# A feed-forward input product as 2x2 blocks with seven block products in place of eight, in a one-core encoder kernel

## The chip, the core and the metric

The kernel runs on one core of a Trainium2 chip. A core has TensorE (PE, matrix products; its weight loads are listed as PEld), VectorE (DVE), ScalarE (ACT), GpSimd (POOL) and SyncE (SP), which run their own instruction lists in order and wait for each other through semaphores. SP issues plain loads and stores; POOL issues, besides its arithmetic, the transfers that add to what lies at the destination. Products accumulate in PSUM banks of 128 x 512 fp32. The metric is the device time of one execution in microseconds (us).

## The reference, cut to what matters

Two layers. Each has a token mixer, a cross-attention and a SwiGLU feed-forward, each followed by a layer norm of ALPHA * x plus the branch. The change touches the norm after the cross-attention and the feed-forward:

```python
D_MODEL, SEQ, DEPTH = 1024, 512, 2
FFN_HIDDEN = 2816

def swiglu_ffn(x, w_in, w_down):          # x (512, 1024)
    gu = x @ w_in                         # w_in (1024, 2 * 2816)
    g, up = gu[..., :FFN_HIDDEN], gu[..., FFN_HIDDEN:]
    return (jax.nn.silu(g) * up) @ w_down
...
        y = memory_cross_attention(x, mem, xa_w_q[l], xa_w_kv[l], xa_w_o[l])
        x = layer_norm(ALPHA * x + y, ln2_g[l], ln2_b[l])
        y = swiglu_ffn(x, ffn_w_in[l], ffn_w_down[l])
        x = layer_norm(ALPHA * x + y, ln3_g[l], ln3_b[l])
```

## The kernel before

All products are fp32 made of three products of rounded parts: each operand is split into `hi` (rounded to fp32r) and `lo` (the rest), and `mm3` issues hi x hi, hi x lo and lo x hi into one PSUM region (lines 250 to 252, so these three lines carry nearly all matmuls).

**The input product of the feed-forward** is 44 blocks a layer (22 gates and 22 ups, alternating). A `Block` has 128 hidden columns: its weights are one tile of 128 x 1024, eight pieces of 128 x 128 that stand in the array while the transposed activations `xT` (128 x 512 tokens) stream through. A block is 8 x 3 = 24 matmuls of 512 columns into one bank. Its weights come in four steps (`added_weights`, lines 282 to 290): SP loads the raw tile, ScalarE rounds it to `whi`, ScalarE writes -`whi` to `wlo`, and a POOL transfer adds the raw weights from DRAM onto `wlo`. The first three blocks make `lo` on VectorE instead (`split`). After a gate ScalarE takes its tanh and VectorE combines; after an up VectorE writes the product to `hid`.

**Buffers.** `wring` has 7 `whi` and 7 `wlo` tiles (RING), `rawp` 3 raw tiles, `big` 26 tiles of 4 KB a partition (x, xT, hid, gains and others), `s2` 9 scratch tiles. PSUM: 4 `accb` banks, and 4 more that `psb` hands out in turn (3 `psb`, 1 `convb`). A tile's slot is fixed when the kernel is built, and whoever writes a slot first waits for the last reader of the tile before it.

**The tail of the cross-attention** (`tail`, lines 509 to 531) adds the last output products to x token tile by token tile (4 tiles of 128), norms, and transposes x on TensorE: two groups of four 128 x 128 transposes a tile, each split by ScalarE and VectorE into `xTh` and `xTl`. x stays in SBUF until the norm after the feed-forward. The first halves (256 tokens) of three blocks are computed between the last transposes.

**The order.** In these stages the instructions' order on each engine is chosen when the kernel is built, by the tool's list scheduler, from the order in which the code is written and the tool's own estimates; at run time each engine follows its list strictly.

After the input product comes the output product of the feed-forward (`wlo<-in_fdn`, `hs`), 22 steps of 24 matmuls of 512 columns, which reads its weights in the same four steps.

## Time and profile before

| | |
|---|---|
| median of 3 runs | 1489.69 us (1489.43 to 1490.8) |
| the profiled execution | 1493.32 us, its span 1491.4 us |
| PE busy | 1453.1 us, 97% |
| DVE, ACT, POOL busy | 47%, 48%, 31% |
| HBM | 213.31 MB read, 8.39 MB written |

Busy times are of the whole span and average over stages with different limits: what the change is worth is read from the stage of the input product, which a layer has once. Where an engine's idle time is named, the releaser behind the arrow is what ended it. Matmuls overlap in the records: what counts for their rate is the distance between two starts, not the duration of one.

### The profile page before, as it was taken

Reading aid. Unit: us, or ns where it says so; the run is one execution under the profiler, and the core shown is the slowest. Engines: PE = TensorE matmul, PEld = TensorE weight load, DVE = VectorE, ACT = ScalarE, POOL = GpSimd, SP = SyncE. Lnnn points to the kernel's source line nnn. Section 1 sums busy time; section 2 is a strip of 40 time slices with the busy share of each in tenths; the row PEclk is TensorE's granted clock in tenths of the full one; section 3 lists DMA queues with packets and bytes.
Section 4 is the critical chain, followed back from the end, with each engine's and each line's share of the span. In section 5 each row is a group of like instructions: output and inputs, shape, how many; then the busy total and the mean of one; then the engine's idle time right before and its main releaser. Section 6 shows DMA issues by size and latency. Waiting matters only on the chain.

```text
span 1491.4 us, 21169 instructions
## 1 busy us (share of the span) xinstructions
PE 1453.1 (97%) x8152; PEld 1256.3 (84%) x8152; DVE 707.6 (47%) x1187; ACT 721.8 (48%) x1278; POOL 466.8 (31%) x665
## 2 busy tenths in 40 slices
PE   8799999999999999999999999999999999999997
PEld 7699988987988888888889999888889888888886
DVE  6999677665511111220469886685663111114005
ACT  3667773453544444553146777624525444446430
POOL 2679771000311111111148877410012111111111
PEclk9899999999999999999999999999999999999999
DMA  5325444242598888998433444423419888889871
GB/s 179 127 70 171 114 128 156 78 161 73 141 223 193 193 196 192 221 201 193 118 116 122 130 127 127 156 71 100 156 48 236 196 190 194 194 193 219 196 140 57
DMA packets 64452, 227.27 MB, mean 152 GB/s; under 512 B 7328, under 2 KB 7360, under 8 KB 64352
## 3 DMA queue, kind: packets, MB, share of 16 engines
q1 hardware_dynamic: 43616, 150.75, 31.1%
q0 software_dynamic: 20736, 75.17, 27.8%
q8 instruction: 64, 1.05, 0.3%
q14 instruction: 36, 0.29, 0.1%
HBM read 213.31 MB, written 8.39 MB: 149 GB/s over the span
## 4 chain that ended last, share of the span: by engine, by line
PE 75%; DVE 12%; ACT 5%; DMA 4%; POOL 3%; issue 1%; SPq 0%; POOLq 0%; DVEq 0%; ACTq 0%
PE accb L250 18%; PE accb L251 18%; PE accb L252 18%; PE psb L250 5%; PE psb L251 5%; PE psb L252 5%; DVE convb L628 3%; DMA raw<-in_xo 3%; DVE wlo L226 1%; DVE p L858 1%; DMA raw<-in_xq 1%; ACT whi L225 1%; PE convb L250 1%; PE convb L252 1%; PE convb L251 1%
## 5 line engine op out<-in xcount | busy, mean ns | idle before, releaser
L250 PE MATMUL accb<-xTh,whi 128*128 128x512 f32 (+1 forms) x1104 | 400.6, 365 | 1.5 <-ACT whi L225 1.3
L251 PE MATMUL accb<-xTl,whi 128*128 128x512 f32 (+1 forms) x1104 | 401.0, 364 | 0.5 <-DVE xTl L432 0.5
L252 PE MATMUL accb<-xTh,wlo 128*128 128x512 f32 (+1 forms) x1104 | 400.3, 363 | 0.1
L287 ACT CAST whi<-raw 128x1024 fp32r<-128x1024 f32 x126 | 132.7, 1055 | 339.4 <-PE accb L251 255.6
L250 PEld LDWEIGHTS accb<-xTh,whi 128*128 128x128 f32 x1104 | 208.7, 190 | 35.7 <-ACT xTh L429 2.7
L251 PEld LDWEIGHTS accb<-xTl,whi 128*128 128x128 f32 x1104 | 209.9, 190 | 32.9 <-DVE xTl L432 1.7
L252 PEld LDWEIGHTS accb<-xTh,wlo 128*128 128x128 f32 x1104 | 209.7, 190 | 32.5 <-DVE wlo L226 0.4
L289 POOL DMA_DIRECT2D wlo<-in_fin x82 | 71.0, 866 | 345.9 <-ACT wlo L288 336.6
L322 POOL TENSOR_TENSOR wlo<-raw,whi 128x1024 fp32r<-128x1024 f32 (+1 forms) x63 | 152.3, 2420 | 62.1 <-ACT whi L314 61.9
L1098 DVE SCALAR_TENSOR_TENSOR scr<-scr,accb 128x512 f32<-128x512 f32 x44 | 30.3, 688 | 253.4 <-ACT scr L1097 253.4
L628 DVE SCALAR_TENSOR_TENSOR convb<-ch,hvec,convb 128x511 f32<-128x511 f32 (+9 forms) x180 | 132.3, 735 | 5.2 <-ACT convb L625 1.7
L288 ACT ACTIVATE wlo<-whi 128x1024 fp32r<-128x1024 f32 x126 | 133.2, 1057 | 2.2
L226 DVE TENSOR_TENSOR wlo<-raw,whi 128x1024 fp32r<-128x1024 f32 (+1 forms) x49 | 56.5, 1158 | 127.2 <-ACT whi L225 126.4
L446 POOL TENSOR_SCALAR ve<-mv 128x1 f32<-128x1 f32 x32 | 27.5, 859 | 244.5 <-DVE mv L467 235.4
L289 POOL DMA_DIRECT2D wlo<-in_fdn x44 | 38.0, 863 | 198.4 <-ACT wlo L288 193.1
L1100 DVE SCALAR_TENSOR_TENSOR hid<-scr,accb 128x512 f32<-128x512 f32 x44 | 30.2, 687 | 136.7 <-PE accb L252 136.7
L225 ACT CAST whi<-raw 128x1024 fp32r<-128x1024 f32 (+1 forms) x49 | 48.9, 1002 | 84.9 <-PE accb L252 33.3
L619 POOL TENSOR_TENSOR cs<-cs,scr 128x511 f32<-128x511 f32 (+29 forms) x60 | 71.5, 1191 | 35.7 <-ACT scr L617 34.5
L314 ACT CAST whi<-raw 128x1024 fp32r<-128x1024 f32 (+1 forms) x63 | 66.7, 1060 | 4.6 <-PE accb L252 1.7
L250 PE MATMUL accb<-whi,hs 128*128 128x512 f32 x176 | 68.6, 390 | 0.0
L251 PE MATMUL accb<-wlo,hs 128*128 128x512 f32 x176 | 68.5, 389 | 0.0
L252 PE MATMUL accb<-whi,hs 128*128 128x512 f32 x176 | 68.5, 389 | 0.0
(295 smaller groups left out, 3165.8 us busy)
## 6 DMA issues: line engine op xcount, KB each, us to landing
raw<-in_fin SPq DMA_DIRECT2D x88, 512.0 KB, 3.6
wlo<-in_fin POOLq DMA_DIRECT2D x82, 512.0 KB, 5.6
raw<-in_fdn SPq DMA_DIRECT2D x44, 512.0 KB, 4.1
wlo<-in_fdn POOLq DMA_DIRECT2D x44, 512.0 KB, 5.9
raw<-in_xk SPq DMA_DIRECT2D x16, 512.0 KB, 3.6
raw<-in_xv SPq DMA_DIRECT2D x16, 512.0 KB, 3.6
raw<-in_wo SPq DMA_DIRECT2D x16, 512.0 KB, 3.6
raw<-in_xq SPq DMA_DIRECT2D x16, 512.0 KB, 3.6
```

What stands on the lines that cost most here:

```text
L225: nc.scalar.copy(hi, src)
L226: nc.vector.tensor_tensor(lo, src, hi.bitcast(F32), op=ALU.subtract)
L250: nc.tensor.matmul(o, l[0], r[0], start=first, stop=False)
L251: nc.tensor.matmul(o, l[0], r[1], start=False, stop=False)
L252: nc.tensor.matmul(o, l[1], r[0], start=False, stop=last)
L287: nc.scalar.copy(hi[:, :1024], raw[:, :1024])
L288: nc.scalar.activation(lo[:, :1024], hi[:, :1024].bitcast(F32), AF.Copy, scale=-1.0)
L289: nc.gpsimd.dma_start(out=lo[:, :1024], in_=src, accum_op=ALU.add)
L314: nc.scalar.copy(hi, raw)
L322: eng.tensor_tensor(lo, raw, hi.bitcast(F32), op=ALU.subtract)
L619: nc.gpsimd.tensor_tensor(o[:, d:], o[:, d:], part, op=ALU.add)
L628: nc.vector.scalar_tensor_tensor(out=o[:, d:], in0=src[:, :SEQ - d], scalar=tap(m, d), in1=o[:, d:], op0=ALU.mult, op1=ALU.add)
```

## The change

Let the weights of one gate block and its up block be the left matrix (2 x 2: gate and up, by the two halves of the 1024 inputs) and the activations the right matrix (2 x 2: the two halves of the inputs, by the two halves of the 512 tokens). The eight block products become seven (Strassen's scheme in Winograd's form). Each of the seven is 4 pieces x 3 = 12 matmuls of 256 columns. In place of the 22 gates and 22 ups there are 22 `Pair`s:

- `load_gate` brings the gate tile in as `added_weights` did (products "11" and "12"); `load_rest` loads the up tile, makes the sums `s1` to `s4` on VectorE, splits them on ScalarE and VectorE into ring tiles, and takes the half "22" by a POOL transfer of 256 KB. A pair takes three and a half ring tiles: the gate, (s3, s2), (22, s1), and half of one for s4.
- `p1`, `p2`, `p3`, `p67`, `p45` are the seven products. `p67` goes to a `psb` bank `w`; VectorE adds `one` (the first product, copied by ScalarE) and `u`; `p45` then overwrites `w`, and VectorE assembles the gate in the bank `v` and the up in `hid`.
- `Halves` keeps seven combinations of the activations, each transposed and split: 14 groups of four transposes a layer in place of 8. They are 14 `big` tiles in place of 8 for `xT`.
- x is stored to DRAM (`xm`) by POOL in the tail of the cross-attention and loaded again by SP for the norm after the feed-forward.
- `load_gate` returns early only if "11" is still there. At step 0 `pairs[2].load_gate(keep=True)` comes after p1 of pair 2 has used "11" up, so the gate of pair 2 is loaded a second time and its p2 is computed a second time.

```diff
--- before.py
+++ after.py
@@ -529,6 +529,153 @@
         blocks[2].first(xT)
         transpose_x(x[3], 3, xT)
         return xT
+    class Halves:
+        def __init__(self):
+            self.parts = {}
+        def put(self, name, src, t):
+            if name not in self.parts:
+                self.parts[name] = (bigt([P, 4, 256], name="xsh"), bigt([P, 4, 256], name="xsl"))
+            pt = psb()
+            for k in range(4):
+                nc.tensor.transpose(pt[:, blk(k)], src[:, blk(k)], ident)
+            hi, lo = (v[:, :, blk(t % 2)] for v in self.parts[name])
+            split(pt.rearrange("p (k c) -> p k c", c=P), hi, lo)
+        def first(self, x, t):
+            self.put("11", x[t][:, 0:512], t)
+            self.put("21", x[t][:, 512:1024], t)
+        def second(self, x, t):
+            b11, b21, b12, b22 = (x[i][:, blk(h, 512)] for i in (t, t + 2) for h in range(2))
+            t1, t2, t3, t4 = (scr(name="tsum")[:, :512] for _ in range(4))
+            nc.vector.tensor_tensor(t3, b22, b12, op=ALU.subtract)
+            self.put("t3", t3, t)
+            nc.vector.tensor_tensor(t1, b12, b11, op=ALU.subtract)
+            nc.vector.tensor_tensor(t2, b22, t1, op=ALU.subtract)
+            self.put("t2", t2, t)
+            nc.vector.tensor_tensor(t4, b21, t2, op=ALU.subtract)
+            self.put("t4", t4, t)
+            self.put("t1", t1, t)
+            self.put("22", b22, t)
+    class Pair:
+        spare = None
+        def __init__(self, gate, up):
+            self.gate, self.up, self.ops, self.raw, self.v = gate, up, {}, None, None
+        def load_gate(self, keep=False):
+            if "11" in self.ops:
+                return
+            raw = fetch(self.gate)
+            hi = wring.tile([P, 1088], F32R, name="whi")
+            lo = wring.tile([P, 1088], F32R, name="wlo")
+            nc.scalar.copy(hi[:, :1024], raw[:, :1024])
+            nc.scalar.activation(lo[:, :1024], hi[:, :1024].bitcast(F32), AF.Copy, scale=-1.0)
+            nc.gpsimd.dma_start(out=lo[:, :1024], in_=self.gate, accum_op=ALU.add)
+            for i, name in enumerate(("11", "12")):
+                self.ops[name] = view((hi[:, blk(i, 512)], lo[:, blk(i, 512)]), "p (k c) -> p k c", c=P)
+            if keep:
+                self.raw = raw
+        def load_rest(self):
+            a = fetch(self.gate) if self.raw is None else self.raw
+            b = fetch(self.up)
+            a0, a1, b0, b1 = a[:, 0:512], a[:, 512:1024], b[:, 0:512], b[:, 512:1024]
+            s1, s2_, s3, s4 = (scr(name="ssum")[:, :512] for _ in range(4))
+            nc.vector.tensor_tensor(s1, b0, b1, op=ALU.add)
+            nc.vector.tensor_tensor(s2_, s1, a0, op=ALU.subtract)
+            nc.vector.tensor_tensor(s3, a0, b0, op=ALU.subtract)
+            nc.vector.tensor_tensor(s4, a1, s2_, op=ALU.subtract)
+            for group in ((("s3", s3), ("s2", s2_)), (("22", b1), ("s1", s1)), (("s4", s4),)):
+                free = Pair.spare if len(group) == 1 else None
+                w = free or (wring.tile([P, 1088], F32R, name="whi"), wring.tile([P, 1088], F32R, name="wlo"))
+                if len(group) == 1:
+                    Pair.spare = None if free else w
+                for i, (name, src) in enumerate(group):
+                    hi, lo = (v[:, blk(1 if free else i, 512)] for v in w)
+                    if name == "22":
+                        nc.scalar.copy(hi, src)
+                        nc.scalar.activation(lo, hi.bitcast(F32), AF.Copy, scale=-1.0)
+                        nc.gpsimd.dma_start(out=lo, in_=self.up[:, 512:1024], accum_op=ALU.add)
+                    else:
+                        split(src, hi, lo)
+                    self.ops[name] = view((hi, lo), "p (k c) -> p k c", c=P)
+            self.raw = None
+        def product(self, o, w, xs_):
+            for k in range(4):
+                mm3(o, cut(self.ops[w], ALL, k, ALL), cut(xs_.parts[PARTNER.get(w, w)], ALL, k, ALL), k == 0, k == 3)
+            del self.ops[w]
+        def p1(self, xs_):
+            self.v = accb()
+            self.product(self.v[:, 0:256], "11", xs_)
+            self.one = scr(name="one")[:, :512]
+            nc.scalar.copy(self.one[:, 0:256], self.v[:, 0:256])
+        def p2(self, xs_):
+            self.product(self.v[:, 0:256], "12", xs_)
+        def p3(self, xs_):
+            self.product(self.v[:, 256:512], "s4", xs_)
+        def p67(self, xs_):
+            self.w, self.u = psb(), scr(name="u")[:, :512]
+            w, u, h0, h1 = self.w, self.u, slice(0, 256), slice(256, 512)
+            self.product(w[:, h1], "s2", xs_)
+            self.product(w[:, h0], "s3", xs_)
+            nc.vector.tensor_tensor(u[:, h0], w[:, h1], self.one[:, h0], op=ALU.add)
+            nc.vector.tensor_tensor(u[:, h1], w[:, h0], u[:, h0], op=ALU.add)
+        def p45(self, xs_, dst):
+            w, u, v, h0, h1 = self.w, self.u, self.v, slice(0, 256), slice(256, 512)
+            self.product(w[:, h0], "22", xs_)
+            self.product(w[:, h1], "s1", xs_)
+            nc.vector.tensor_tensor(self.one[:, h1], w[:, h1], u[:, h0], op=ALU.add)
+            nc.vector.tensor_tensor(dst.rearrange("p (a c) -> p a c", a=2), w.rearrange("p (a c) -> p a c", a=2),
+                                    u[:, h1].rearrange("p (a c) -> p a c", a=1).broadcast_to([P, 2, 256]), op=ALU.add)
+            nc.vector.tensor_tensor(v, v, self.one, op=ALU.add)
+            th = scr()[:, :512]
+            nc.scalar.activation(th, v, AF.Tanh, scale=0.5)
+            nc.vector.scalar_tensor_tensor(out=th, in0=th, scalar=1.0, in1=v, op0=ALU.add, op1=ALU.mult)
+            nc.vector.scalar_tensor_tensor(out=dst, in0=th, scalar=0.5, in1=dst, op0=ALU.mult, op1=ALU.mult)
+    PARTNER = {"12": "21", "s4": "22", "22": "t4", "s1": "t1", "s2": "t2", "s3": "t3"}
+    EARLY = 3
+    def tail_pairs(x, gb, half0, mm, pairs, keep):
+        xs_ = Halves()
+        for t in range(NT):
+            if t < EARLY:
+                pairs[t].load_gate()
+            norm = Norm(x[t], gb)
+            o = mm(t)
+            for i, y in enumerate(half0(t) + o):
+                norm.half(i, y)
+            if t >= 2:
+                xs_.first(x, t - 2)
+            norm.finish(lambda rows, cols: keep(t, rows, cols))
+        pairs[0].p1(xs_)
+        xs_.second(x, 0)
+        pairs[1].p1(xs_)
+        pairs[0].p2(xs_)
+        pairs[2].p1(xs_)
+        xs_.second(x, 1)
+        pairs[1].p2(xs_)
+        pairs[2].p2(xs_)
+        return xs_
 
     mkv = [dram.tile([XH, P, 1024], F32, name=f"mkv{l}") for l in range(DEPTH)]
@@ -1082,24 +1229,37 @@
                 mm3(o, cut(yx[k], ALL, blk(t)), cut(w1[k // 2], ALL, k % 2, ALL), k == 0, k == KD - 1)
             return [o]
-        return tail(x, gb, lambda t: [o0[t]], second_half, nxt), nxt
+        def keep(t, rows, cols):
+            nc.gpsimd.dma_start(out=xm[blk(t), cols], in_=rows)
+        return tail_pairs(x, gb, lambda t: [o0[t]], second_half, nxt, keep), nxt
 
     def ffn_blocks(l):
-        return [Block(fin[l, (j % 2) * NJ + j // 2], added=j >= 3) for j in range(2 * NJ)]
-    def ffn(l, x, xT, blocks, keep):
+        return [Pair(fin[l, j], fin[l, NJ + j]) for j in range(NJ)]
+    def ffn(l, xs_, pairs, keep):
         last = l == DEPTH - 1
         hid = [bigt([P, 2, SEQ], F32, name="hid") for _ in range(NJ // 2)]
+        def dst(j):
+            return hid[j // 2][:, j % 2, :]
+        pairs[0].load_rest()
+        pairs[1].load_rest()
         for j in range(NJ):
-            og = blocks[2 * j].done(xT)
-            th = scr()[:, :512]
-            nc.scalar.activation(th, og, AF.Tanh, scale=0.5)
-            nc.vector.scalar_tensor_tensor(out=th, in0=th, scalar=1.0, in1=og, op0=ALU.add, op1=ALU.mult)
-            ou = blocks[2 * j + 1].done(xT)
-            nc.vector.scalar_tensor_tensor(out=hid[j // 2][:, j % 2, :], in0=th, scalar=0.5, in1=ou,
-                                           op0=ALU.mult, op1=ALU.mult)
+            if j + 2 < NJ:
+                pairs[j + 2].load_gate(keep=True)
+                pairs[j + 2].load_rest()
+            pairs[j].p67(xs_)
+            if j + 1 < NJ and pairs[j + 1].v is None:
+                pairs[j + 1].p1(xs_)
+            if "12" in pairs[j].ops:
+                pairs[j].p2(xs_)
+            pairs[j].p3(xs_)
+            pairs[j].p45(xs_, dst(j))
         gb = load_gb(l, 2)
+        x = load_x(xm)
         o = [[accb() for _ in range(NT)], [psb() for _ in range(NT)]]
         def operands(j):
@@ -1128,6 +1288,7 @@
         return tail(x, gb, lambda t: [], finish, nxt, keep), nxt
     xs = dram.tile([SEQ, D], F32, name="xs")
+    xm = dram.tile([SEQ, D], F32, name="xm")
     blocks = mixer_blocks(0)
     x = []
     for t in range(NT):
@@ -1148,7 +1309,7 @@
         rope_tables()
     for l in range(DEPTH):
         x, xT, blocks = mixer(l, xT, blocks, x_in if l == 0 else xs)
-        xT, blocks = cross(l, x, xT, blocks)
+        halves, pairs = cross(l, x, xT, blocks)
         def keep(t, rows, cols):
             if l == DEPTH - 1:
@@ -1156,7 +1317,7 @@
             else:
                 nc.gpsimd.dma_start(out=xs[blk(t), cols], in_=rows)
-        xT, blocks = ffn(l, x, xT, blocks, keep)
+        xT, blocks = ffn(l, halves, pairs, keep)
 
 # ---- launch: one core; host code lays the arrays out and nothing else ----
```

**ScalarE, a step in the middle of the input product.** The first piece is before: one gate and one up, each a rounding cast (L287) and the negative copy (L288), and the tanh (L1097).

```order
L287 CAST whi_5197<-raw_5195 128x1024 [waits DMAHW0_49,PE_49]
L1097 ACTIVATE scr_4988<-accb_4963 128x512 [waits PE_49]
L288 ACTIVATE wlo_5198<-whi_5197 128x1024 [waits DMASW3_49,Activation_49]
L287 CAST whi_5230<-raw_5228 128x1024 [waits DMAHW1_49,PE_49]
L288 ACTIVATE wlo_5231<-whi_5230 128x1024 [waits DMASW4_49,PE_49,Activation_49]
```

The second is the change: L582 and L583 bring in the gate of pair 8 (whi_5628), L650 is the tanh of pair 5, then come pair 8's s2, s3, the half 22 and s1, the copy `one` of pair 7, and pair 8's s4 and pair 9's gate.

```order
L582 CAST whi_5628<-raw_5626 128x1024 [waits DMAHW6_49,PE_49]
L583 ACTIVATE wlo_5629<-whi_5628 128x1024 [waits DMASW0_49,PE_49,Activation_49]
L650 ACTIVATE scr_5622<-accb_5426 128x512 [waits DVE_49]
L225 CAST whi_5643<-ssum_5636 128x512 [waits DVE_49,PE_49]
L225 CAST whi_5643<-ssum_5637 128x512 [waits DVE_49]
L607 CAST whi_5649<-raw_5633 128x512 [waits DMAHW7_49,PE_49]
L225 CAST whi_5649<-ssum_5635 128x512
L608 ACTIVATE wlo_5650<-whi_5649 128x512 [waits DMASW2_49,PE_49,Activation_49]
L624 COPY one_5701<-accb_5688 128x256
L225 CAST whi_5656<-ssum_5638 128x512 [waits DVE_49,PE_49]
L582 CAST whi_5760<-raw_5758 128x1024 [waits DMAHW0_49,PE_49]
```

Two casts and two copies of 1024 a step became one of each and six of 512, and the casts still wait for TensorE to be done with a slot.

**TensorE, the start of p1 of pair 7 and of p67 of pair 7 (change).** accb_5688 is the bank `v` and psb_5790 the bank `w` of pair 7; DMASW is a POOL transfer.

```order
L250 MATMUL accb_5688<-xsh_4570,whi_5498 128x256 [waits Activation_49]
L251 MATMUL accb_5688<-xsl_4571,whi_5498 128x256
L250 MATMUL psb_5790<-xsh_4681,whi_5513 128x256 [waits Activation_49]
L251 MATMUL psb_5790<-xsl_4682,whi_5513 128x256
L252 MATMUL accb_5688<-xsh_4570,wlo_5499 128x256 [waits DMASW3_49]
L250 MATMUL accb_5688<-xsh_4570,whi_5498 128x256
```

Before, a block's matmuls stood alone in the list; now those of several pairs are woven, and the one that waits for the added `wlo` stands ahead of the others.

**VectorE in a step.** The first piece is before: two instructions a step, one for the gate and one for the up.

```order
L1098 SCALAR_TENSOR_TENSOR scr_5260<-scr_5260,accb_5235 128x512 [waits Activation_49]
L1100 SCALAR_TENSOR_TENSOR hid_4775<-scr_5260,accb_5270 128x512 [waits DVE_49,PE_49]
L1098 SCALAR_TENSOR_TENSOR scr_5328<-scr_5328,accb_5303 128x512 [waits Activation_49]
L1100 SCALAR_TENSOR_TENSOR hid_4776<-scr_5328,accb_5338 128x512 [waits DVE_49,PE_49]
L1098 SCALAR_TENSOR_TENSOR scr_5396<-scr_5396,accb_5371 128x512 [waits Activation_49]
```

The second is the change, 12 of the 15 instructions of a step: convb_5528 is `w` of pair 5, accb_5426 its `v`; ssum_5635 to ssum_5638 are s1 to s4 of pair 8.

```order
L637 TENSOR_TENSOR u_5529<-convb_5528,one_5439 128x256
L226 TENSOR_TENSOR wlo_5395<-ssum_5508,whi_5394 128x512 [waits Activation_49]
L638 TENSOR_TENSOR u_5529<-convb_5528,u_5529 128x256 [waits DVE_49]
L645 TENSOR_TENSOR one_5439<-convb_5528,u_5529 128x256 [waits PE_49]
L646 TENSOR_TENSOR hid_4829<-convb_5528,u_5529 128x512 [waits DVE_49]
L648 TENSOR_TENSOR accb_5426<-accb_5426,one_5439 128x512 [waits DVE_49]
L595 TENSOR_TENSOR ssum_5635<-raw_5633 128x512 [waits DMAHW7_49]
L651 SCALAR_TENSOR_TENSOR scr_5622<-scr_5622,accb_5426 128x512 [waits Activation_49]
L596 TENSOR_TENSOR ssum_5636<-ssum_5635,raw_5626 128x512 [waits DMAHW6_49,DVE_49]
L652 SCALAR_TENSOR_TENSOR hid_4829<-scr_5622,hid_4829 128x512 [waits DVE_49]
L597 TENSOR_TENSOR ssum_5637<-raw_5626,raw_5633 128x512
L598 TENSOR_TENSOR ssum_5638<-raw_5626,ssum_5636 128x512 [waits DVE_49]
```

The list now holds a wait for TensorE (L645, p45 of pair 5) right behind the instruction (L638) that p45 itself waits for.

## Rows read from the trace of the kernel before

**Rows 1.** Busy time in the input product's two stretches, by engine, with clock and DMA share.

```profile
381.07:631.20 250.13, 250.07 (x1186) 210.04 (x1184) 46.35 (x75) 115.20 (x139) 45.93 (x54) 1.00 0.88 200
1113.00:1363.10 250.10, 250.03 (x1185) 209.96 (x1184) 46.33 (x75) 115.18 (x139) 45.39 (x53) 1.00 0.88 200
```

**Rows 2.** Timeline of TensorE, matmuls of 512 columns: start, duration.

```profile
470.04 0.39 PE L250 MATMUL accb<-xTh,whi 128*128 128x512 f32 x1
...
470.72 0.39 PE L250 MATMUL accb<-xTh,whi 128*128 128x512 f32 x1
```

**Rows 3.** Timeline of TensorE, matmuls of 256 columns.

```profile
396.02 0.28 PE L250 MATMUL accb<-xTh,whi 128*128 128x256 f32 x1
...
397.94 0.28 PE L251 MATMUL accb<-xTl,whi 128*128 128x256 f32 x1
```

**Rows 4.** Timeline of the tail: transposes, and where VectorE is then.

```profile
381.07 0.60 PE L426 MATMUL convb<-ident,x 128*128 128x128 f32 x4
381.27 0.69 DVE L462 SCALAR_TENSOR_TENSOR x<-x,psb 128x512 f32<-128x512 f32 x1 [0.42 <-PE psb L252]
```

**Rows 5.** Timeline in the input product: from a block's last matmul to the added weights' issue.

```profile
478.43 0.39 PE L251 MATMUL accb<-xTl,whi 128*128 128x512 f32 x1
...
478.85 1.05 ACT L287 CAST whi<-raw 128x1024 fp32r<-128x1024 f32 x1 [2.95 <-PE accb L251]
...
479.94 1.06 ACT L288 ACTIVATE wlo<-whi 128x1024 fp32r<-128x1024 f32 x1
...
481.29 0.86 POOL L289 DMA_DIRECT2D wlo<-in_fin  x1 [4.23 <-ACT wlo L288]
```

**Rows 6.** POOL's line 289, stretch 1430 to 1450: issue to landing.

```profile
DMA to landing us min/median/max: 5.3/5.3/5.8
```

**Rows 7.** Busy times where only these transfers run; DMA share and GB/s last.

```profile
1440.00:1445.00 5.00, 5.00 (x24) 4.14 (x23) 0.00 (x0) 1.68 (x3) 0.86 (x1) 1.00 0.52 84
```

**Rows 8.** Groups by line: VectorE and ScalarE instructions of the sizes that the change issues.

```profile
L226 DVE TENSOR_TENSOR hs<-hid,hs 128x512 fp32r<-128x512 f32 x44 | 28.7, 688 | 19.4 <-ACT hs L225 19.2
L225 ACT CAST hs<-hid 128x512 fp32r<-128x512 f32 x44 | 25.1, 616 | 2.0 <-DVE hs L226 2.0
L1097 ACT ACTIVATE scr<-accb 128x512 f32<-128x512 f32 x44 | 25.9, 590 | 0.0
L432 DVE TENSOR_TENSOR xTl<-psb,xTh 128x256 fp32r<-128x256 f32 x64 | 24.1, 413 | 31.2 <-ACT xTh L429 31.0
```

**Rows 9.** Timeline of VectorE in the tail: the aggregate, and the norm that waits for POOL.

```profile
377.27 0.21 DVE L467 BATCH_NORM_AGGREGATE mv<-st 128x2 f32<-128x12 f32 x1
377.51 1.28 DVE L471 SCALAR_TENSOR_TENSOR x<-x,mv,gb 128x1024 f32<-128x1024 f32 x1
...
379.57 1.28 DVE L473 SCALAR_TENSOR_TENSOR x<-x,rstd,gb 128x1024 f32<-128x1024 f32 x1 [0.77 <-POOL rstd L450]
```

**Rows 10.** DMA issues: count, size, microseconds to landing.

```profile
raw<-in_fin SPq DMA_DIRECT2D x88, 512.0 KB, 3.6
```

**Rows 11.** TensorE around its longest wait: timeline, then windows (PE busy first, PEclk third from last).

```profile
60.65 1.11 PE L549 MATMUL psb<-ident,mem 128*128 128x128 f32 x4 [8.93 <-DMA mem<-in_mem]
...
51.70:54.00 2.30, 0.02 (x1) 0.00 (x0) 2.30 (x5) 2.29 (x5) 1.09 (x2) 1.00 0.00 0
54.00:54.50 0.50, 0.00 (x0) 0.00 (x0) 0.50 (x1) 0.38 (x1) 0.50 (x1) 0.86 0.00 0
...
64.50:65.00 0.50, 0.50 (x3) 0.40 (x2) 0.50 (x2) 0.00 (x0) 0.50 (x1) 0.90 0.45 131
```

**Rows 12.** The end of the span, where TensorE has nothing left to do.

```profile
1483.00:1484.00 1.00, 0.00 (x0) 0.00 (x0) 0.97 (x2) 0.00 (x0) 0.00 (x0) 1.00 0.40 160
...
1487.00:1488.00 1.00, 0.00 (x0) 0.00 (x0) 1.00 (x2) 0.00 (x0) 0.00 (x0) 0.98 0.00 0
```

**Rows 13.** Timeline of TensorE at the start, 256 columns at the low clock.

```profile
12.07 0.41 PE L250 MATMUL accb<-xTh,whi 128*128 128x256 f32 x1
...
13.99 0.41 PE L250 MATMUL accb<-xTh,whi 128*128 128x256 f32 x1
```

## The prediction

> **What bounds the kernel now.** I read the engines' busy times of the stretch that is changed, then the distance between matmuls, then the path of a weight tile from load to use.
>
> The input product lasts 250.1 us in either layer; TensorE is busy for all of it, while ScalarE is busy 115 us, VectorE and POOL 46 each, at full clock [rows 1]. So the rate of matmuls is the bound, and the other engines' waits cost nothing. Three intervals of 512-column matmuls take 0.68 us, 0.2267 each [rows 2]; sixteen of 256 columns take 1.92, 0.120 each [rows 3]. Half the columns cost 53%, not 50%.
>
> **The change, part by part.** *TensorE alone.* A pair loses 48 matmuls of 512 (10.88 us) and gets 84 of 256 (10.08): -0.80, times 22 = -17.6 a layer. The second p2 of pair 2 gives back 12 x 0.12 = 1.4, six more groups of transposes at 0.60 [rows 4] give back 3.6. Three blocks of before were already computed in halves of 256, each 48 x 0.120 - 24 x 0.2267 = 0.32 dearer, so another 0.9 goes. That would be 13.5 us a layer won if TensorE stayed the bound. I don't think it does; three chains have to be held against 10.08 us a step.
>
> *Ring and POOL transfer (the chain I expect to bind).* The ring has 7 tiles and a pair takes 3.5. Once the scheme is in steady state, all seven are held when pair j's gate is to be cast, so its cast (L582) waits for the last matmul that reads the oldest: for even j the end of p45 of pair j-3; for odd j a p2 that stands 6 matmuls (0.72 us) later in the list. From there, by the path of a tile today: ScalarE starts 0.03 after the matmul's end (478.43 + 0.39, 478.85), the negative copy starts 1.09 later and takes 1.06, POOL issues 0.29 after that [rows 5]. Before, this latency lay behind other blocks' matmuls. Landing took 5.3 where only such transfers ran [rows 6], with DMA 52% busy [rows 7], about what the change leaves per us. Sum 0.03 + 1.09 + 1.06 + 0.29 + 5.3 = 7.77. On TensorE's list the matmul that waits for this landing (third line of p1, L252) stands ahead of the rest of p1, p67, p2 and p45. From it to the end of the next p45 there are 48 matmuls (rest of p1 10, p67 9, p2 5, p45 24) or, for odd pairs, 53 (10, 12, 7, 24): 0.120 each, and 0.16 for the last, whose duration is 0.28 [rows 3]. That p45 frees the slot of the next gate but one in the ring's turn, so it closes the chain: **13.69** us for an even step (7.77 + 48 x 0.12 + 0.16), **15.01** for an odd one (7.77 + 0.72 + 53 x 0.12 + 0.16), 14.35 on average against 10.88 before. No work fills this: after a p45, TensorE has 27 to 32 matmuls that don't need the landing, then only two of p1 and two of p67.
>
> *VectorE.* A step gives it 12 instructions of 512 columns (s1 to s4, four low parts, hid, the sum into v, two around the tanh) and 3 of 256. At 0.70 (688 ns and the gap) and 0.42 [rows 8] that is 9.7. L645 stands right behind L638 and waits for p45, which itself waits for L638: 24 x 0.12 + 0.16 + 0.1 of hops = 3.1 in which VectorE can do nothing else, with L646 and the next pair's sums queued behind. With 0.2 of waiting for the tanh, which stands behind a gate's cast and copy, 13.0 a step. This is over 10.08 too, but under 14.35. ScalarE has 2 x 1.06, six of 512 at 0.6 and about 1 more: 6.7, no bound.
>
> *The head of the stretch.* From VectorE's place at 381.27 [rows 4] to the low part of s2 of pair 0 its list has 31 instructions of 512 (21.7), two aggregates (0.4), four norm steps of 1024 at 1.28 and one wait of 0.77 for POOL [rows 9]: 28.1, thus 409.4. TensorE has done its early products by about 403 and waits some 6 us. Then 19 x 0.70 + 2 x 0.42 = 14.1, and twice 0.8 for raw tiles whose buffer s4 frees late and whose load takes 3.6 [rows 10], bring u of pair 0 to 425.1; its p45 ends at 428.2, which is 47.1 after 381.07.
>
> *Sum of a layer.* 47.1; pairs 1 and 2 at VectorE's 13.0 = 26.0; 17 steps of the ring chain (9 odd, 8 even) 244.6; pairs 20 and 21, nothing more to load, 53 and 46 matmuls, 6.4 + 5.5; the hand-over to the output product, whose first hs cast stands on ScalarE behind a cast and a copy that wait for the last p45, and behind the tanh: 1.06 + 1.06 + 0.59 + 0.6 + 0.69 and hops = 4.2. Together 333.8 against 250.1: +83.7, two layers **+167**.
>
> *Clock.* Each step of 14.4 us then has some 4.2 us in which TensorE has next to nothing. What such holes do, the trace shows only for longer ones: the last matmul ended 0.02 into 51.70 to 54.00, at 51.72, the clock was still full there, and the mean 0.86 of 54.0 to 54.5 puts the fall to half at about 54.4, 2.7 us after the matmul; work began again at 60.65 and the clock was back at 64.6, 4.0 us later [rows 11]. Against that, at the end no matmul runs from 1483.0, and the clock falls only within 1487 to 1488 [rows 12]. So the hole lies between the two. At half clock 256-column matmuls stand 0.213 apart [rows 13]: 4.0 us hold 19 of them, which would take 2.25, so a fall costs 1.75. Bounds: none, or one in each of 19 steps (33 a layer). I take half, 16.6 a layer, **+33** for two.
>
> *Costed at nothing.* x to DRAM and back: four POOL issues of 0.86 [rows 5] while POOL is idle, and a reload that has 22 x 24 x 0.2267 = 120 us of output product to hide it; without that cover 4 x 3.6 = 14. PSUM: v and w come free a step ahead of use. The up tile's raw load starts 6.8 after a p45 and lands 3.6 later; the sums need it at about 17. If it came late, VectorE's chain would grow by what is missing.
>
> *A page against the rows.* The landing is the largest term: 5.3 here, 3.6 for a plain load of the same 512 KB. The Trainium skill, "DMA: Bandwidth & Descriptors", section "Anatomy of one DMA — SWDGE (gpsimd) path", gives a GpSimd-issued transfer as about 2.0 us plus bytes over 436 GB/s; by it 512 KB would take an estimated 3.2. The rows on this kernel's own transfers disagree, and the measurement decides. By the page's figure the ring chain would be some 12.25 a step, VectorE's would be the longer one, and the time that of rival (c), about 1610.
>
> **The rivals.**
> (a) *Faster: TensorE stays the bound.* In its favour: each engine's busy sum is under 10.08 a step, and today's schedule hides all such latencies. Then a layer gives 250.1 - 13.5 and the kernel about **1463**. It decides where both chains fall under 10.08: the slot would have to come free 4.3 us earlier and VectorE's chain be 3 us shorter. Both are orders fixed at build time.
> (b) *In between*: the head as computed, steps of 10.5 to 12.5 because VectorE's instructions are cheaper here and landings shorter. A layer is 47.1 + 19 steps + 16.1 = 263 to 301, the kernel **1515 to 1590**.
> (c) *VectorE binds*: a landing like a plain load's 3.6 puts the ring chain at 12.65 on average, so 13.0 a step holds: 47.1 + 19 x 13.0 + 16.1 = 310, +60 a layer, and shorter holes, so no fall: **1610**.
> (d) *Ring chain, clock holds*, as at the end of the span: +167, **1657**.
> (e) *Ring chain, the clock falls in half the steps*: **1690**.
> (f) *It falls in every step*: **1724**; slower matmuls also sit inside the chain.
>
> **How the numbers follow.** The profiled execution took 1493.3 (span 1491.4 and 1.9 around it). 1493.3 + 167 + 33 = 1693, and that execution stands 3.6 above the median of 1489.7, so **1690**. Chances: (a) 0.04, (b) 0.06, (c) 0.15, (d) 0.25, (e) 0.30, (f) 0.20. Leaving out (a), (b) and a little beyond (f), the range is **1600 to 1735**. 0.2% (3 us) is about what a measurement of this kernel can tell from no change: faster by more 0.04, within 0.01, slower by more 0.95.
>
> **What would show it.** In the stretches TensorE's busy share falls to about 70%; each step has an idle time of some 4 us ended by the added `wlo` (POOL's L584) ahead of an L252, 13.7 and 15.0 us apart in turn. ScalarE's L582 waits for TensorE, VectorE's L645 waits about 3 us. TensorE idles some 6 us ahead of p67 of pair 0 and 4 ahead of the first hs product. The stretch lasts 334, or up to 367 with a granted clock under 1. If the idle time is instead ended by VectorE (u ahead of p45), the answer is (c); a stretch of some 237 with TensorE fully busy is (a). I would be wrong on the ring if L582 didn't wait, wrong on the landing if it took 3 to 4 us, wrong on the head if p45 of pair 0 ended far from 47 us after the stretch's start.

## The result, and the profile after

1773.03 us median (1769.79 to 1773.27) against 1490.24 of before: ratio 1.189, interval 1.187 to 1.191. The forecast was 1690, its range 1600 to 1735. The direction, the place and the chain are as forecast; the time lies 38 us above the range. The profiled execution has a span of 1771.2.

The page: TensorE's busy time, and its granted clock over the 40 slices.

```profile
PE 1542.5 (87%) x9664; PEld 1402.2 (79%) x9664; DVE 1032.9 (58%) x1765; ACT 810.4 (46%) x1504; POOL 479.9 (27%) x681
...
PEclk9899999999787877889999999999988878788999
```

TensorE was 97% busy before. Apart from the second slice, those with 7 and 8 are the two input products: there the clock is not at full speed, while in [rows 1] it was. Windows of the first layer (PE busy first, PEclk third from last): the head up to the first p45, most of the steps, the hand-over to the output product, and the first matmuls behind it.

```profile
381.07:427.90 46.83, 39.54 (x281) 36.35 (x280) 38.02 (x60) 22.43 (x39) 10.25 (x12) 0.96 0.42 127
...
468.40:747.75 279.35, 215.70 (x1387) 209.18 (x1387) 135.89 (x241) 99.94 (x161) 27.68 (x32) 0.80 0.44 106
...
760.40:769.92 9.52, 0.01 (x1) 0.00 (x0) 2.15 (x4) 6.10 (x8) 2.48 (x4) 0.73 1.04 349
...
769.92:775.00 5.08, 5.08 (x12) 3.89 (x13) 5.08 (x10) 5.08 (x11) 0.68 (x2) 0.51 1.06 278
```

From 381.07 to the first matmul of the output product at 769.92 are 388.9 us, where before had 250.1. In the steps TensorE is 77% busy, VectorE 49% and ScalarE 36%: no engine is full. The chain of one step, where TensorE, ScalarE, POOL and the landing take turns (timeline; the releaser stands in brackets):

```profile
491.35 0.28 PE L251 MATMUL accb<-xsl,whi 128*128 128x256 f32 x1
...
491.67 1.05 ACT L582 CAST whi<-raw 128x1024 fp32r<-128x1024 f32 x1 [0.22 <-PE accb L251]
...
492.75 1.06 ACT L583 ACTIVATE wlo<-whi 128x1024 fp32r<-128x1024 f32 x1
...
494.11 0.86 POOL L584 DMA_DIRECT2D wlo<-in_fin  x1 [11.09 <-ACT wlo L583]
...
496.38 0.39 PE L250 MATMUL psb<-xsh,whi 128*128 128x256 f32 x1 [1.40 <-ACT whi L225]
...
499.41 0.58 PE L252 MATMUL accb<-xsh,wlo 128*128 128x256 f32 x1 [2.53 <-DMA wlo<-in_fin]
```

The slot's last reader ends at 491.63, the cast starts 0.04 later, the copy 1.08 after that, POOL issues at 494.11, and TensorE goes on at 499.41, when the low part has landed: 7.78 us, where the prediction had 7.77 from [rows 5, 6]. The clock around such a hole, from windows:

```profile
482.30:488.10 5.80, 5.80 (x27) 5.80 (x28) 0.51 (x2) 0.00 (x0) 0.72 (x1) 0.50 0.66 191
488.10:494.99 6.89, 6.89 (x57) 6.68 (x56) 3.48 (x7) 3.22 (x4) 0.86 (x1) 0.99 0.00 0
494.99:499.41 4.42, 0.50 (x2) 0.30 (x2) 4.42 (x9) 3.17 (x6) 0.06 (x1) 0.89 0.83 164
```

In a hole of 4.4 us with two matmuls the mean is 0.89, so the clock falls about 1 us before the hole ends; then 27 matmuls take 5.8 us at 0.50, 0.213 each, and only then 57 run at 0.120. Steps follow from the starts of VectorE's L645, which waits for each p45:

```profile
490.95 0.42 DVE L645 TENSOR_TENSOR one<-psb,u 128x256 f32<-128x256 f32 x1 [8.10 <-PE psb L252]
...
508.64 0.43 DVE L645 TENSOR_TENSOR one<-convb,u 128x256 f32<-128x256 f32 x1 [8.02 <-PE convb L252]
...
525.03 0.42 DVE L645 TENSOR_TENSOR one<-psb,u 128x256 f32<-128x256 f32 x1 [8.15 <-PE psb L252]
```

17.69 and 16.39 in turn. Last the hand-over to the output product:

```profile
756.18 2.33 SPq L412 DMA_DIRECT2D x<-xm  x4
...
758.61 26.02 SPq L266 DMA_DIRECT2D raw<-in_fdn  x4
...
762.40 1.05 ACT L287 CAST whi<-raw 128x1024 fp32r<-128x1024 f32 x1 [4.16 <-DMA raw<-in_fdn]
...
766.74 1.05 ACT L287 CAST whi<-raw 128x1024 fp32r<-128x1024 f32 x1 [1.39 <-DMA raw<-in_fdn]
...
768.78 0.58 ACT L650 ACTIVATE scr<-accb 128x512 f32<-128x512 f32 x1
...
769.92 0.80 PE L250 MATMUL accb<-whi,hs 128*128 128x512 f32 x1 [9.52 <-ACT hs L225]
```

The four loads of x stand ahead of output weights on SP's queue, with the DMA engines full (share 1.04 above). ScalarE's cast waits for those weights, and behind it stand the last tanh and the first hs cast. TensorE waits 9.5 us and comes back at the low clock: its next 12 matmuls of 512 take 5.08 us in place of 2.72.

### The profile page after: what moved, and what is told of

It is laid out like the page before. It is cut to its first block, busy times and chain, and to the rows that moved or that the text cites. A ratio compares the mean times of both kernels' runs of the same rounds, so it can differ in the third digit from the quotient of the medians.

```text
span 1771.2 us, 25166 instructions
## 1 busy us (share of the span) xinstructions
PE 1542.5 (87%) x9664; PEld 1402.2 (79%) x9664; DVE 1032.9 (58%) x1765; ACT 810.4 (46%) x1504; POOL 479.9 (27%) x681
## 4 chain that ended last, share of the span: by engine, by line
PE 37%; issue 36%; DVE 11%; POOL 6%; DMA 6%; ACT 4%; POOLq 0%; SPq 0%; DVEq 0%; ACTq 0%
PE accb L250 7%; PE accb L252 6%; PE accb L251 6%; PE psb L250 4%; PE psb L251 4%; PE psb L252 4%; DVE convb L775 2%; DMA raw<-in_xo 2%; POOL wlo L609 2%; POOL wlo L584 2%; DMA raw<-in_fdn 1%; DVE wlo L226 1%; DVE p L1005 1%; DMA raw<-in_xq 1%; ACT whi L225 1%
## 5 line engine op out<-in xcount | busy, mean ns | idle before, releaser
L252 PE MATMUL accb<-xsh,wlo 128*128 128x256 f32 x536 | 180.6, 337 | 103.1 <-DMA wlo<-in_fin 103.1
L252 PEld LDWEIGHTS accb<-xsh,wlo 128*128 128x128 f32 x536 | 125.9, 235 | 110.5 <-DMA wlo<-in_fin 110.5
L250 PE MATMUL psb<-xsh,whi 128*128 128x256 f32 x512 | 163.6, 320 | 39.0 <-ACT whi L225 39.0
L250 PE MATMUL accb<-xsh,whi 128*128 128x256 f32 x536 | 173.5, 325 | 1.3 <-ACT one L624 0.9
L251 PE MATMUL accb<-xsl,whi 128*128 128x256 f32 x536 | 173.0, 323 | 0.7 <-DVE xsl L226 0.7
L252 PE MATMUL psb<-xsh,wlo 128*128 128x256 f32 x512 | 160.2, 313 | 7.9 <-DVE wlo L226 7.9
L251 PE MATMUL psb<-xsl,whi 128*128 128x256 f32 x512 | 159.8, 312 | 0.0
L645 DVE TENSOR_TENSOR one<-psb,u 128x256 f32<-128x256 f32 x32 | 13.6, 425 | 231.1 <-PE psb L252 231.1
L250 PEld LDWEIGHTS accb<-xsh,whi 128*128 128x128 f32 x536 | 126.4, 236 | 2.2 <-ACT one L624 1.3
L251 PEld LDWEIGHTS accb<-xsl,whi 128*128 128x128 f32 x536 | 125.8, 235 | 1.1 <-DVE xsl L226 1.1
L582 ACT CAST whi<-raw 128x1024 fp32r<-128x1024 f32 x46 | 48.4, 1053 | 169.6 <-PE convb L251 69.8
L250 PE MATMUL accb<-xTh,whi 128*128 128x256 f32 (+1 forms) x352 | 118.2, 340 | 1.4 <-ACT whi L225 1.3
```

The costliest lines, as they stand in the source:

```text
L250: nc.tensor.matmul(o, l[0], r[0], start=first, stop=False)
L251: nc.tensor.matmul(o, l[0], r[1], start=False, stop=False)
L252: nc.tensor.matmul(o, l[1], r[0], start=False, stop=last)
L582: nc.scalar.copy(hi[:, :1024], raw[:, :1024])
L645: nc.vector.tensor_tensor(self.one[:, h1], w[:, h1], u[:, h0], op=ALU.add)
```

## The experiments

All times are medians; ratios are to the kernel before. Where not said otherwise the edit is to the changed kernel.

**Is it the ring?** First theory: the late slot and the 7.8 us behind it. Rivals: VectorE's list, or the transfers themselves.

```diff
-BIG = 26
+BIG = 25
...
+    half4 = ctx.enter_context(tc.tile_pool(name="half4", bufs=1))
...
                 if len(group) == 1:
-                    Pair.spare = None if free else w
+                    w = (half4.tile([P, 512], F32R, name="fhi"), half4.tile([P, 512], F32R, name="flo"))
```

> s4 gets a half tile of its own (4 KB, taken from one of the 26 big tiles), so a pair takes 3 of the 7 ring tiles and not 3.5; the adding transfer stays with its 5.3 us. By the list the gate's cast then waits for the last matmul of a p67 and its p1 stands 86 matmuls (10.3 us) later, so the landing is covered. Ring theory: VectorE's 13.0 us a step binds, 1610 to 1650, or about 1700 if holes of 3 us a step still make the clock fall each time. Rival, the landing itself or the transfers' rate is the bound wherever the slot comes from: a step stays at 16 to 17 us, 1750 or more. Rival, VectorE sets the 17 us: no change.

1598.7 us, ratio 1.072 (1.069 to 1.075), 11 us under the range expected. The 17 steps are 12.0 us each, all alike, at full clock:

```profile
465.18:668.98 203.80, 179.33 (x1430) 173.01 (x1429) 144.30 (x255) 105.43 (x171) 29.35 (x34) 1.00 0.62 153
```

The transfers and VectorE's instructions are the same as in the change. That rules out VectorE's work and the landing as a bound of 17 us wherever the slot comes from. It doesn't show the slot alone, since with other buffers the order of TensorE's list was chosen otherwise too. The next run keeps the buffers.

```diff
-        for j in range(NJ):
+        with issue_order(tc, (ET.PE,)):
+            for j in range(NJ):
```

> The change with TensorE's instructions held in the order in which the code is written (p67 of a pair, p1 of the next, p2, p3, p45), all buffers, transfers and other engines' work as in the change. The gate's slot then comes free at the end of a p67, and its p1 is reached a whole step later. Theory that the list's order closes the ring chain: nothing waits for the landing any more, steps of 11 to 12 us as with s4 in its own tile, 1590 to 1620. Rival, seven tiles are too few in any order: steps stay over 14 us, 1690 or more.

1574.5, ratio 1.057 (1.055 to 1.059), 16 us under the range expected. Two steps, and the hand-over:

```profile
543.49:554.23 10.74, 10.34 (x86) 10.13 (x85) 9.26 (x16) 6.60 (x12) 1.73 (x2) 1.00 0.57 132
554.23:565.96 11.73, 10.60 (x86) 10.19 (x85) 7.97 (x15) 5.68 (x10) 1.73 (x2) 1.00 0.83 193
657.00:670.00 13.00, 9.57 (x75) 8.93 (x74) 4.57 (x10) 9.05 (x12) 3.01 (x4) 1.00 1.04 309
```

Most steps are 10.7 and 11.6 in turn, at full clock. With the same seven tiles, holding TensorE in the written order is worth 199 us. Some of it is at the hand-over, where TensorE now waits 3.4 us in place of 9.5. The lists of ScalarE and VectorE came out a little otherwise too (the tanh, for one, stands elsewhere). In the order as chosen, p1's start and its wait for the landing stood ahead of p67 and the p45 that frees the next slot. The rival on seven tiles falls.

```diff
-            nc.scalar.activation(lo[:, :1024], hi[:, :1024].bitcast(F32), AF.Copy, scale=-1.0)
-            nc.gpsimd.dma_start(out=lo[:, :1024], in_=self.gate, accum_op=ALU.add)
+            nc.gpsimd.tensor_tensor(lo[:, :1024], raw[:, :1024], hi[:, :1024].bitcast(F32), op=ALU.subtract)
```

> The gate's low part is made by GpSimd from the raw tile in SBUF (raw minus whi), in place of ScalarE's negative copy and the adding transfer; nothing else changes. Ring theory (a gate's slot comes free late, and cast, copy, issue and landing, 7.8 us, then hold up p1 and with it the next p45): the low part is there about 1.05 + 2.4 = 3.5 us after the slot, 4.3 us sooner, so the ring chain drops under VectorE's 13.0 us a step; 19 steps of 13 to 14 in place of 17.1 are 60 to 78 us a layer, so 1617 to 1650 in place of 1773, less if the clock still falls in each step. Rival, VectorE's own list or the order of matmuls sets 17 us a step: no more than 10 us gained, since POOL was idle and none of their work is taken away.

1674.6, ratio 1.125 (1.120 to 1.131): 98 us gained, 25 short of the least expected. In the first layer the steps are 12.9 and 14.3, as expected, and the clock fell in one of 17. In the second it fell in ten of 17, and the same steps took 14.3 and 16.5. Windows over the 17 steps of each layer:

```profile
456.60:690.11 233.51, 186.16 (x1434) 175.78 (x1433) 175.35 (x257) 90.42 (x155) 55.32 (x34) 0.99 0.33 96
1269.34:1519.46 250.12, 204.11 (x1434) 193.29 (x1433) 175.36 (x257) 90.39 (x155) 55.33 (x34) 0.90 0.31 90
```

So 17 of the missing 25 us are the clock again, although TensorE's waits are alike in both layers: three in a step, of 0.4 to 1.2 us each. The timeline shows where they come from:

```profile
552.49 1.05 ACT L582 CAST whi<-raw 128x1024 fp32r<-128x1024 f32 x1 [3.94 <-PE convb L251]
...
553.63 2.38 POOL L583 TENSOR_TENSOR wlo<-raw,whi 128x1024 fp32r<-128x1024 f32 x1 [4.68 <-DVE hid L645]
...
554.15 2.41 DVE L594 TENSOR_TENSOR ssum<-raw 128x512 f32<-128x512 f32 x1
...
556.07 0.39 PE L252 MATMUL accb<-xsh,wlo 128*128 128x256 f32 x1 [0.37 <-POOL wlo L583]
...
560.23 0.38 PE L252 MATMUL psb<-xsh,wlo 128*128 128x256 f32 x1 [1.18 <-DVE wlo L226]
```

The low part is there 3.6 us after the slot, as expected, and TensorE waits 0.4 us for it. But the sum s1 (L594), which took 0.68 in the change, took 2.41 beside POOL's subtraction, and with it s2 and TensorE's next waits came late. The Trainium skill, "SBUF — State Buffer", section "Who interferes with whom", says that a VectorE instruction with two inputs in SBUF contends with a GpSimd instruction that reads SBUF; this row agrees. So the landing was part of the chain, and the waits that are left, with the clock, cost part of the gain. VectorE's list is that of the change, instruction for instruction; TensorE's order came out otherwise.

**Is it the clock?** Extra matmuls fill the hole; their result is overwritten by p3.

```diff
             self.v = accb()
+            for k in range(30):                              # second run: 16
+                nc.tensor.matmul(self.v[:, 256:512], self.ops["11"][0][:, k % 4, :], xs_.parts["11"][0][:, k % 4, :], start=k == 0, stop=k == 29)
```

> Thirty more matmuls of 256 columns (3.6 us) ahead of each p1, into the half of the bank v that p3 starts anew later, so the result is unchanged; they need only whi and so run in the hole in which TensorE waits for the landing. Clock theory: each step now loses 2.5 us because 27 matmuls after the hole run 0.213 apart in place of 0.120; with the hole filled the clock holds, a step takes 14.4 to 15 us in place of 17.1 although TensorE does a third more work, and the kernel 1680 to 1700. Rival, the clock is a side effect and the step's length comes from elsewhere: no gain, or up to 137 us lost (38 steps of 3.6) if the hole was not idle for TensorE's list.

1651.7, ratio 1.108 (1.105 to 1.111): a third more matmuls in the input product, and 121 us faster, more than expected. From the eighth step on, steps are 13.68 = 114 x 0.120, TensorE without a gap:

```profile
570.00:680.00 110.00, 110.00 (x919) 110.00 (x919) 69.83 (x122) 50.94 (x81) 14.11 (x17) 1.00 0.56 136
```

This is not the clock alone: with 30 more matmuls the order was chosen otherwise (p67 whole and ahead of p1), which also frees the slot sooner. Sixteen leave the order as it was:

> As the run with thirty, but sixteen extra matmuls ahead of each p1: here TensorE's list keeps the order of the change (with thirty, the order had moved too: p67 came whole and ahead of p1, and a gate's slot came free sooner). So the clock alone is tested. Clock theory: the hole of some 4 us holds 1.9 us of work, the clock holds, a step is the ring chain at full clock, 14.4 us on average (13.7 and 15.0 in turn) in place of 17.1: 100 us gained, about 1670. If the clock still falls in each step, the step stays at 17.1 and the time within 10 us of 1773. If it falls in some: between.

1713.5, ratio 1.150 (1.148 to 1.152): 60 us gained, not 100. The steps are of two kinds; windows over single steps:

```profile
516.41:531.67 15.26, 12.85 (x107) 12.64 (x106) 9.09 (x16) 6.81 (x12) 1.73 (x2) 1.00 0.49 120
...
606.53:623.39 16.86, 14.34 (x107) 14.14 (x106) 9.09 (x16) 6.81 (x12) 1.73 (x2) 0.90 0.43 110
623.39:637.23 13.84, 11.65 (x97) 11.45 (x96) 7.89 (x15) 5.67 (x10) 1.73 (x2) 1.00 0.55 134
```

Where the clock held, steps are 13.8 and 15.3, close to the forecast 13.69 and 15.01 of the ring chain; where it fell in an otherwise like step (the first two rows), 1.6 us more. TensorE's order is that of the change, its waits for the landing are 2.2 to 2.5 us, and the clock fell in 17 of the 34 ring steps. The theory took filling half the hole to be enough; it wasn't.

**Is the hand-over the reload?**

```diff
-        x = load_x(xm)          # before the output product; now inside its loop, after step j == 9
```

> x is reloaded after ten steps of the output product in place of before it. Theory for the hand-over: the four loads of x stand on SP's queue ahead of the weights of the output product, a cast on ScalarE waits for those weights (4.2 and 1.4 us), and the tanh of the last pair and the first hs cast stand behind that cast; so TensorE's 9.5 us of idle time become about 4 to 5 in each layer, and the clock may not fall: 10 to 16 us gained in all, 1757 to 1763. Rival, the 9.5 us are the tail of the last pair and its casts, which the prediction put at 4.2 with too few instructions: within 3 us of 1773.

1749.1, ratio 1.173 (1.170 to 1.176): 24 us, where 10 to 16 were expected. No part of the 9.5 is left. On this run's timeline the output product starts before VectorE has read the last p45:

```profile
756.45 0.40 PE L250 MATMUL accb<-whi,hs 128*128 128x512 f32 x1
...
756.81 0.42 DVE L645 TENSOR_TENSOR one<-convb,u 128x256 f32<-128x256 f32 x1
```

2 x (9.5 + 2.4 of low clock behind it) = 23.8. TensorE's order is that of the change. ScalarE's list came out otherwise: hs is now cast ahead of the weights' casts that waited, and ahead of the last pair's tanh. How much of the 24 us is the queue and how much this order, the run doesn't show.

**What the narrow matmuls take back.** An edit to the kernel before.

```diff
+            if blocks[2 * j].o is None:
+                blocks[2 * j].first(xT)          # 256 columns; done() then does the other 256. The same for the up block
```

> The kernel before, with every block of the input product of the feed-forward as two halves of 256 columns (three of 44 were so already), otherwise unchanged: 41 more blocks a layer of 48 x 0.120 in place of 24 x 0.2267, +0.32 each. Theory: 26 us more, 1516, if TensorE stays the bound; this is the share of the scheme's gain in products that the narrower matmuls take back. Rival, each half as 0.113 (half of 0.2267): no change, 1490.

1514.3, ratio 1.016 (1.014 to 1.018): +24, where 26 were expected at 0.120 a matmul. Seven products for eight would save 10.88 / 8 = 1.36 us a pair; 84 x (0.120 - 0.1133) = 0.56 of it go to the width, and the 0.80 of the prediction are left.

**What is left when the ring is mended.** The three edits (s4's own tile, the written order, the late reload) together:

> s4 in a half tile of its own, TensorE in the written order and x reloaded after ten steps of the output product, together. Theory: ring chain and hand-over are gone (1599 with s4 alone, 24 us for the reload), and what is left is the head (47 us a layer against 27 or so of TensorE's work) and steps of 10.1 (TensorE) to 12.0 (as with s4 alone): 1530 to 1575. Before's 1490 isn't reached, since the head alone costs some 15 us a layer. Rival, the three fixes overlap: no better than 1590.

1566.9, ratio 1.051 (1.049 to 1.053), steps of 11.33. Its timeline:

```profile
567.24 0.42 DVE L640 TENSOR_TENSOR u<-psb,u 128x256 f32<-128x256 f32 x1
...
567.71 0.39 PE L251 MATMUL psb<-xsh,whi 128*128 128x256 f32 x1 [1.00 <-DVE u L640]
...
570.89 0.43 DVE L647 TENSOR_TENSOR one<-psb,u 128x256 f32<-128x256 f32 x1 [2.63 <-PE psb L253]
```

TensorE waits for VectorE's u, since p45 overwrites the bank that u reads, and VectorE then waits 2.63 us for p45. Two ways to take this apart:

```diff
-            w, u, v, h0, h1 = self.w, self.u, ...           # p45 overwrites p67's bank
+            w, u, v, h0, h1 = psb(), self.u, ...            # own bank (run e9)
...
-            nc.vector.tensor_tensor(s1, b0, b1, op=ALU.add)  # and s2, s3, s4
+            s1, s2_, s3, s4 = b0, b1, a0, a1                # run e10, one bank as in e7
```

> The kernel with s4 in its own half tile, TensorE in the written order and the late reload (1567), and p45 in a PSUM bank of its own in place of overwriting the bank of p67. There a step was 11.33 us: VectorE's instructions 8.7 and 2.6 of waiting for p45, which itself waited 1.0 for VectorE's u. Theory that this mutual wait is what is left: p45 no longer waits for u, a step comes to 10.1 to 10.5 and the kernel to 1525 to 1540. Rival, another wait takes its place at once (a bank that comes free late, the low part of s1): 1555 or more.

> The kernel of 1567 with the four sums of each pair left out: raw halves are rounded and split in their place, so the output is not the reference's. VectorE has 2.8 us less in a step and 5.6 less in the head of each layer. If VectorE's list sets the 11.33 us, the step falls to TensorE's 10.1 and the kernel to 1500 to 1515. If the wait of p45 for u and of VectorE for p45 sets it whatever else VectorE does, the step stays near 11 and only the head is shorter: 1550 to 1556.

With its own bank: 1501.3, ratio 1.008 (1.006 to 1.011), better than expected, steps of 10.08. Without the sums (a kernel that leaves out part of the work): 1514.8, ratio 1.016 (1.015 to 1.018), steps of 10.1 to 10.8. Either cure alone brings the steps to TensorE's 10.08 or near it, so the 11.33 were VectorE's work (8.7) and its wait for p45 (2.6) in one loop. Steps of both runs, and the head of the run with its own bank:

```profile
460.00:640.00 180.00, 180.00 (x1486) 179.27 (x1485) 146.40 (x263) 117.79 (x185) 34.38 (x42) 1.00 0.79 197
...
446.64:621.29 174.65, 173.84 (x1430) 172.12 (x1429) 105.18 (x187) 103.28 (x170) 29.32 (x34) 1.00 0.78 179
...
381.00:436.00 55.00, 45.07 (x317) 41.76 (x316) 47.33 (x74) 26.03 (x46) 12.12 (x14) 0.95 0.45 129
```

The steps are full, or nearly so. In the head of the run with its own bank TensorE idles 10 us a layer, 4.0 of it for one landing and most of the rest for VectorE, which is busy for 47 of 55. Two edits there, on top of that run:

```diff
-            if "11" in self.ops:
+            if "11" in self.ops or self.v is not None:      # no second cast, copy, adding transfer and p2 of pair 2's gate; load_rest still fetches its raw tile
...
-    EARLY = 3
+    EARLY = 4                                               # and, in the second run, p1 and p2 of pair 3 in the tail
```

> The kernel of 1501 (s4 in its own half tile, written order, late reload, p45 in its own bank) without the second load of pair 2's gate and the second p2 of pair 2. TensorE is fully busy in its steps of 10.1 us, so what is left is the head. Theory: 12 matmuls (1.44 us) a layer go, and with them a cast, a copy and a 512 KB transfer ahead of the landing for which TensorE waits 4.0 us in the head: 3 to 10 us gained in all, 1491 to 1498. Rival, the head is VectorE's list alone: the matmuls fall into idle time and nothing is gained, 1501.

> The same with four early pairs in place of three: p1 and p2 of pair 3 (24 matmuls, 2.9 us) run in the head too, where TensorE waits some 6 us for VectorE. Theory: 2 x 2.9 us off the steps behind, done in idle time: 4 to 6 us under the run without the second load, 1485 to 1493, about the time of before. Rival, one more gate in the ring and one more split delays the first pairs' own tiles: no gain or up to 5 us lost against it.

1498.3, ratio 1.0042 (1.0026 to 1.0057), and 1496.4, ratio 1.0033 (1.0023 to 1.0044). The first gain, 3 us, is at the low end of what was expected; the second, 2 us, is below it and not clear of noise, since the intervals overlap. The head of the last run:

```profile
381.00:436.00 55.00, 51.91 (x357) 47.82 (x356) 47.62 (x72) 21.45 (x39) 13.79 (x16) 0.97 0.43 130
```

TensorE idles 3 us in place of 10, but just behind this window it waits 3.2 and 1.3 us for landings: more than half of the idle time only moved. No version beats the kernel before.

## Why the prediction was half right

| a layer, us | predicted | measured in the first |
|---|---|---|
| head, to the end of p45 of pair 0 | 47.1 | 46.6 |
| pairs 1 and 2 | 26.0 | 29.0 |
| 17 steps of the ring chain, without clock | 244.6 | 291.1 with it |
| clock | 16.6 | about 2.5 in each step |
| pairs 20 and 21 | 11.9 | 12.7 |
| hand-over | 4.2 | 9.5, and 2.4 at low clock behind |
| sum | 350.4 | 391.3 |

The difference, 40.9, is 82 us for two layers: the 83 that are missing between 1690 and 1773.

- **TensorE's rate** held: 0.120 for 256 columns, in the changed kernel and in that of before with halves.
- **The ring chain** held to its terms: 7.78 for 7.77, the alternation of even and odd steps (1.3 us apart in the run and in the sum), and, in the run with sixteen extra matmuls, the steps themselves at full clock, 13.8 and 15.3. Experiments on ring and order removed it; with the landing taken out, TensorE's longest wait in a step was 1.2 us.
- **The clock** is the step of the prediction that failed most. The prediction took a fall in half of the steps, 1.75 us each, since [rows 11] showed 4.0 us at half clock. The clock fell in each of the measured ring steps and stayed at half for 5.8 us: 27 x (0.213 - 0.120) = 2.5, 43 us over the 17 steps in place of 15. As said in rival (f), slow matmuls sit inside the chain, and its 33 a layer were still too few because a fall was priced too low.
- **The hand-over** was mis-sized by an edit costed at nothing. The reload of x has 120 us of cover for its own use, which is true; what it delays was not asked: the output weights behind it on SP's queue, the cast that waits for them, and the tanh and hs cast behind that cast. Together with the order that ScalarE's list took, it cost 12 us a layer. Nor was the 4.2 needed that the prediction had there: with the late reload TensorE didn't wait at all, because hs was cast ahead of the tanh.
- **VectorE's 13.0** was too much: its instructions of 512 start about 0.60 apart back to back, not 0.70, and once the ring was mended the steps were 12.0, then 11.3. In the ring steps it didn't bind, so there this cost nothing, but the bounds of rivals (b) and (c) rested on it. In pairs 1 and 2, which the prediction gave to it, TensorE's longest waits were 3.9 us for a landing and 2.9 for a cast, and the clock was 0.89 and 0.75 in their windows (15.5 and 13.5 us).
- **Landing**: 5.3 us again for 512 KB (494.11 to 499.41 above), so the condition of rival (c), a landing of 3.6, didn't come about. The estimate of 3.2 by the Trainium skill, "DMA: Bandwidth & Descriptors", section "Anatomy of one DMA — SWDGE (gpsimd) path", isn't what these adding transfers took.

Why the time exceeds the range is thus shown for its two largest terms: moving the reload gives back 24 us, and filling half the hole with TensorE's order unchanged gives back 60, although the clock still fell in half of the steps.

## What to carry to other kernels

A scheme that saves an eighth of the products has little to spend: 0.80 us of 10.88 a pair were left after the narrower matmuls, less than one wait of a microsecond in a step. Over a layer that is 17.6 us, and TensorE's idle time in the head took 10 of it even in a version whose steps were full. When a pool has just enough slots, follow the slot in a circle (last reader, refill, landing, the waiting instruction, what stands behind it on the list); holding TensorE in the written order was worth 199 us with no buffer added. A hole can cost more than its length: behind each of 4.4 us the low clock took 2.5 more. And for a transfer costed at nothing, ask not only when its data are needed but who queues behind it.

## What the runs showed of the hardware

- TensorE's clock, by run and step: with one hole of 4.4 us (two matmuls in it) it was at half for 5.8 us behind the hole, and fell in all 34 ring steps. With one wait of 2.2 to 2.5 us it fell in 17 of 34. With three waits of 0.4 to 1.2 us, 2.6 to 3.0 in all, it fell in one of 17 in the first layer and ten of 17 in the second. With s4 in its own tile, at most 1.8 us idle in a step, it fell in none of 34. Thirty useless matmuls a step made the kernel 121 us faster, partly through the order.
- A VectorE sum of two SBUF operands took 2.41 us in place of 0.68 beside a POOL subtraction from SBUF.
